# Three raw weight buffers, x's first chunk ahead of the first weights, and the last two column blocks computed token-major

## The chip, the core and the metric

The kernel runs on one NeuronCore of a Trainium2 chip: TensorE (PE, with its weight loads shown as PEld), VectorE (DVE), ScalarE (ACT), GpSimd (POOL) and SyncE (SP), which issues most of the DMA transfers. All five work through their own queue of instructions in order and wait for each other on semaphores. The metric is the device time of one execution in microseconds (us). The kernel before takes 1832.29 us, the median of three runs (1831.8 to 1832.62).

## What is computed

A two-layer encoder trunk on 512 tokens of width 1024, all in float32. Each layer mixes the tokens in three ways in parallel (differential attention, a depthwise convolution module, 2-D neighbourhood attention), merges them with sigmoid gates, then applies a gated feed-forward block and a gated per-layer input embedding. Cut to the frame:

```python
for i in range(DEPTH):
    h = rmsnorm(x, norm_mix[i])
    qa, ka, va, glu_in, qc, kc, vc, gates = split(h @ w_in[i])
    ya = diff_attention(qa, ka, va, ...)
    yb = conformer_conv(glu_in, ...)
    yc = neighbourhood_attention(qc, kc, vc, rpb[i])
    x = x + (ga * (ya @ w_br_a[i]) + gb * (yb @ w_br_b[i]) + gc * (yc @ w_br_c[i])) @ w_o[i]
    h = rmsnorm(x, norm_ffn[i])
    x = x + (silu(h @ w_ffn_gate[i]) * (h @ w_ffn_up[i])) @ w_ffn_down[i]
    h = rmsnorm(x, norm_ple[i])
    x = x + sigmoid(h @ w_ple_gate[i]) * (p[i] @ w_ple_in[i])
return rmsnorm(x, norm_final)
```

## The kernel before

**Layout.** Activations lie channel-major: a chunk is a [128 channels, 512 tokens] tile, and eight chunks make x. A block of 128 output channels is one accumulation in a PSUM bank. Every operand is split into a high part and a low remainder (`split`, L160: an ACT copy to the rounded type, then a DVE subtraction), and each product is three matmuls, high x high, high x low, low x high (`mm3`, L173; the three lines are L175 to L177). A full block is 8 chunks x 3 matmuls of 512 columns.

**Weights.** `weights` (L164) loads one block of up to 512 KB into a raw tile (tag `wr`, two buffers) from SP's queue, then splits it into `wh` and `wl` (three buffers each). A new load into `wr` waits until DVE's subtraction has read the raw tile that held the buffer before. The loads are put early in the program by a raised priority (`w_ahead`), and a scheduler orders the instructions of every engine but PE, whose order is written out by hand. SP's queue is strictly in order: what stands behind a waiting load waits too. Beside the weights it carries the biases, the rope tables and the small copies that `stack` (L611) makes inside the chip to build the stacked operands (`natten_qk`, `natten_x`, `diff_qk`) of the attention scores.

**Opening** (`opening`, L307). Ten warm-up matmuls on zeros run while the first data arrives. Then the first four blocks of the convolution's input are computed chunk by chunk (k = 0 to 7), so that x and the weights may arrive in pieces: weight columns 0 to 255 (for k = 0 and 1) in tiles `t`, 256 to 511 in `rp`, 512 to 1023 in `e`. x's chunk 0 and 1 are issued from ACT's queue (L315, L317), the rest and all weight pieces from SP's. For k = 0, `operand` (L257) makes the high part on ACT and the low one on DVE.

**Middle.** Neighbourhood attention (`natten_in`, `natten_unit`), differential attention, gates and convolution run interleaved; the convolution's 31 taps are DVE work placed between. Scratch tiles have the tag `t` (8 buffers), row tiles (broadcast norms, rope tables) the tag `r` (4).

**End** (`ple`, L949, and `final`, L995). In the last layer the blocks m = 0 to 6 of the gated embedding are computed channel-major; then `final` does block 7 in two halves of 256 tokens. PE turns the finished chunks, scaled by the final gain, back to token-major (`turn`, four transposes a time). Sums of squares per token are matmuls with a column of ones (`total`), the root is a POOL power (`column`), and DVE and ACT scale the turned tiles into one row tile for each 128 tokens, which SP stores with one 512 KB transfer (`store`, L1046).

## Time and profile before

| what | value |
|---|---|
| median of the runs | 1832.29 us (1831.8 to 1832.62) |
| the profiled execution, its own time | 1832.66 us |
| its span, first to last instruction | 1830.6 us |
| granted TensorE clock, mean | 0.998 |
| HBM read, written | 180.79 MB, 7.34 MB |
| DMA busy, hardware queue 1 | 37.5% of 16 engines |
| POOL busy | 23.6 us (1%) |
| costliest group: PE L175 `ffn_mm<-wo_h,ffn_wh`, 704 matmuls | 274.2 us |
| costliest on DVE: the convolution's taps, L158 `conv_z` | 179.4 us (240 x 748 ns) |
| costliest on ACT: the split L141 `ffn_wh<-ffn_wr` | 144.0 us (152 x 949 ns) |

The span is 2.1 us shorter than the execution's own time; the rest lies around it. In the views, a row of the timeline begins with the start and the duration in us, then engine, line, operation and tiles (`out<-in`), then how often; in square brackets stands the idle time before it and what ended it. In the views of waits the numbers are the total in us, how often, and the longest. A matmul's duration covers its way through the array, so consecutive matmuls overlap: what one costs is the distance between two starts. A window's row gives the busy time of PE, PEld, DVE, ACT and POOL, the granted PE clock, the DMA share and GB/s.

### The profile page before, as it was taken

To read this page: it belongs to the slowest core of one execution; us is meant where nothing else is said; L and a number is where in the kernel's file an instruction comes from. 1 tells how busy PE (TensorE), PEld (TensorE's weight loads), DVE (VectorE), ACT (ScalarE), POOL (GpSimd) and SP (SyncE) were. 2 spreads that over 40 slices of the span, in tenths; PEclk is the share of its full clock that TensorE was granted. 3 is DMA by queue.
4 is the path that set the end of the run, shared out by engine and by line. 5 is a ranking of instruction groups with operands and counts; after the bars stand their busy time and mean duration, and the time that the engine had idled before them with its cause. 6 is when DMAs were issued, how large, how long until landed. Compare 5 with 4: busy or idle time off the path is not lost.

```text
span 1830.6 us, 23574 instructions
## 1 busy us (share of the span) xinstructions
PE 1815.6 (99%) x8796; PEld 1524.3 (83%) x8796; DVE 1190.5 (65%) x1917; ACT 764.8 (42%) x1330; POOL 23.6 (1%) x56
## 2 busy tenths in 40 slices
PE   9999999999999999999999999999999999999998
PEld 7888888888888888888888888888878888888887
DVE  6888887887644434445777878888775444344455
ACT  5476555325432222233535755552353322232344
POOL 0000000000000000000000000000000000000000
PEclk9999999999999999999999999999999999999999
DMA  5565541334422232223436655322353222322232
GB/s 176 176 191 167 144 135 41 109 101 156 146 98 99 82 102 103 99 81 113 152 121 203 183 156 145 103 75 93 107 193 104 99 97 79 117 92 99 84 107 102
DMA packets 88225, 221.13 MB, mean 121 GB/s; under 512 B 12080, under 2 KB 19376, under 8 KB 88112
## 3 DMA queue, kind: packets, MB, share of 16 engines
q1 hardware_dynamic: 87536, 218.94, 37.5%
q8 instruction: 70, 1.15, 0.2%
q10 hardware_dynamic: 576, 0.69, 0.1%
q14 instruction: 43, 0.35, 0.1%
HBM read 180.79 MB, written 7.34 MB: 103 GB/s over the span
## 4 chain that ended last, share of the span: by engine, by line
PE 93%; DVE 2%; DMA 2%; ACT 2%; issue 1%; DVEq 0%; ACTq 0%; SPq 0%; POOLq 0%; POOL 0%
PE ffn_mm L175 13%; PE ffn_mm L177 13%; PE ffn_mm L176 13%; PE mergea_mm L176 2%; PE mergea_mm L175 2%; PE mergea_mm L177 2%; PE diff_sc L757 2%; PE gatec_mm L175 2%; PE gatec_mm L176 2%; PE gatec_mm L177 2%; PE ple_mm L177 2%; PE ple_mm L175 2%; PE ple_mm L176 2%; PE wo_mm L176 2%; PE wo_mm L177 2%; PE diff_mm L175 2%
## 5 line engine op out<-in xcount | busy, mean ns | idle before, releaser
L141 ACT ACTIVATE ffn_wh<-ffn_wr 128x1024 fp32r<-128x1024 f32 (+1 forms) x152 | 144.0, 949 | 513.9 <-issue 367.8
L175 PE MATMUL ffn_mm<-wo_h,ffn_wh 128*128 128x512 f32 x704 | 274.2, 390 | 0.0
L177 PE MATMUL ffn_mm<-wo_h,ffn_wl 128*128 128x512 f32 x704 | 273.9, 389 | 0.0
L176 PE MATMUL ffn_mm<-wo_h,ffn_wh 128*128 128x512 f32 x704 | 273.9, 389 | 0.0
L155 DVE TENSOR_TENSOR ffn_wl<-ffn_wr,ffn_wh 128x1024 fp32r<-128x1024 f32 (+1 forms) x152 | 164.7, 1085 | 129.2 <-ACT ffn_wh L141 129.2
L158 DVE SCALAR_TENSOR_TENSOR conv_z<-glu_z,pre_par,conv_z 128x512 f32<-128x512 f32 x240 | 179.4, 748 | 3.0
L177 PEld LDWEIGHTS ffn_mm<-wo_h,ffn_wl 128*128 128x128 f32 x704 | 132.1, 188 | 27.5
L176 PEld LDWEIGHTS ffn_mm<-wo_h,ffn_wh 128*128 128x128 f32 x704 | 132.1, 188 | 27.4
L175 PEld LDWEIGHTS ffn_mm<-wo_h,ffn_wh 128*128 128x128 f32 x704 | 132.1, 188 | 27.3
L155 DVE TENSOR_TENSOR ffn_t<-ffn_t,ffn_mm 128x512 f32<-128x512 f32 x44 | 30.3, 688 | 114.8 <-PE ffn_mm L177 114.8
L155 DVE TENSOR_TENSOR ffn_t<-ffn_mm,wo_r 128x512 f32<-128x512 f32 x44 | 30.4, 691 | 110.3 <-PE ffn_mm L177 110.3
L141 ACT ACTIVATE mergea_wh<-mergea_wr 128x1024 fp32r<-128x1024 f32 (+1 forms) x32 | 27.1, 848 | 96.6 <-PE mergea_mm L176 70.8
L175 PE MATMUL ffn_mm<-ffn_z,ffn_wh 128*128 128x512 f32 x160 | 62.2, 389 | 0.0
L176 PE MATMUL ffn_mm<-ffn_z,ffn_wh 128*128 128x512 f32 x160 | 62.2, 389 | 0.0
L177 PE MATMUL ffn_mm<-ffn_z,ffn_wl 128*128 128x512 f32 x160 | 62.2, 389 | 0.0
L175 PE MATMUL ffn_mm<-ffn_y,ffn_wh 128*128 128x512 f32 x160 | 62.2, 389 | 0.0
L176 PE MATMUL ffn_mm<-ffn_y,ffn_wh 128*128 128x512 f32 x160 | 62.2, 389 | 0.0
L177 PE MATMUL ffn_mm<-ffn_y,ffn_wl 128*128 128x512 f32 x160 | 62.2, 389 | 0.0
L141 ACT ACTIVATE diff_a<-diff_sc,diff_s 128x512 f32<-128x512 f32 x32 | 22.0, 689 | 61.8 <-DVE diff_s L848 61.8
L848 DVE TENSOR_REDUCE diff_s<-diff_sc 128x1 f32<-128x512 f32 x64 | 41.9, 685 | 5.9 <-PE diff_sc L757 5.8
L155 DVE TENSOR_TENSOR wo_x<-wo_x,ffn_mm 128x512 f32<-128x512 f32 x32 | 22.0, 687 | 31.5 <-PE ffn_mm L177 31.5
L141 ACT ACTIVATE natten_wh<-natten_wr 128x1024 fp32r<-128x1024 f32 x24 | 25.4, 1056 | 37.4 <-issue 18.0
(583 smaller groups left out, 4628.6 us busy)
## 6 DMA issues: line engine op xcount, KB each, us to landing
ffn_wr<-w_fg SPq DMA_DIRECT2D x44, 512.0 KB, 3.2
ffn_wr<-w_fu SPq DMA_DIRECT2D x44, 512.0 KB, 3.1
ffn_wr<-w_fd SPq DMA_DIRECT2D x32, 512.0 KB, 3.4
natten_wr<-w_in SPq DMA_DIRECT2D x16, 512.0 KB, 3.7
natten_b<-bias SPq DMA_DIRECT2D x32, 256.0 KB, 3.3
diff_wr<-w_in SPq DMA_DIRECT2D x16, 512.0 KB, 3.5
gatec_wr<-w_in SPq DMA_DIRECT2D x16, 512.0 KB, 4.0
gateb_wr<-w_in SPq DMA_DIRECT2D x16, 512.0 KB, 3.3
```

The source lines that it names most:

```text
L141: i = self.nc.scalar.activation(out, in_, func, **kw)
L155: return self.nc.vector.tensor_tensor(out, a, b, op)
L158: return self.nc.vector.scalar_tensor_tensor(out, a, s, b, op0, op1)
L175: mm(out, wh, ah, start=first, stop=False)
L176: mm(out, wh, al, start=False, stop=False)
L177: mm(out, wl, ah, start=False, stop=last)
L757: self.nc.tensor.matmul(out, st4[:, u, qs], st[:, ks], start=n == 0, stop=n == 1)
L848: nc.vector.tensor_reduce(out=m[:, u:u + 1], in_=sc, op=ALU.max, axis=AX.X, negate=True)
```

## The change

`build`: the raw weight tag `wr` gets three buffers for two, `t` seven for eight, `r` three for four. `opening`: x's chunk 0 is the first transfer of SP's queue; the weight pieces are columns 0 to 127 (k = 0 alone), 128 to 511 (k = 1 to 3) and 512 to 1023; the first of the small pieces, x's chunk 1 and the rest of the parameters go to ACT's queue; `operand` of chunk 1 now stands ahead of the `rp` pieces. `ple`: the last layer's loop stops after block 5, and the new `gains` turns the last two blocks' final gains into rows. `final` computes blocks 6 and 7 together, token-major: the activations (128 tokens) are the stationary operand, and the two blocks' weights, loaded side by side, the moving one of 256 columns; four token tiles follow each other. The sums of squares of the last two blocks come from a DVE reduction along the rows; each row tile is stored in two transfers of 256 KB, one from ACT's queue and one from SP's.

```diff
--- before.py
+++ after.py
@@ -288,8 +288,8 @@
     def build(self):
         nc, tc, a = self.nc, self.tc, self.a
-        self.bufs = dict(wr=2, wh=3, wl=3, h=8, qk=2, kh=2, v=4, pt=2, y=5, z=5, x=4, t=8, rp=4,
-                         e=4, a=3, r=4, ss=1, sm=8, rc=4, b=2, s=8)
+        self.bufs = dict(wr=3, wh=3, wl=3, h=8, qk=2, kh=2, v=4, pt=2, y=5, z=5, x=4, t=7, rp=4,
+                         e=4, a=3, r=3, ss=1, sm=8, rc=4, b=2, s=8)
         self.bg, self.w_ahead = BG, 400
         self.pbufs = dict(mm=3, sc=2, tr=2, av=1)
         with tc.tile_pool(name="sb", bufs=1) as self.pool, \
@@ -310,20 +310,18 @@
         self.parts = self.sb("par", [P, PAR], bufs=1)
         self.small()
         mix = slice(0, KD)
+        xc = [t for _ in range(KD // 2) for t in self.parts_of("x", [512], 2)]
+        nc.sync.dma_start(xc[0], a["xT"][0])
         nc.scalar.dma_start(self.parts[:, mix], a["par"][:, mix])
-        xc = [t for _ in range(KD // 2) for t in self.parts_of("x", [512], 2)]
-        nc.scalar.dma_start(xc[0], a["xT"][0])
         self.consts()
-        nc.scalar.dma_start(xc[1], a["xT"][1])
-        nc.scalar.dma_start(self.parts[:, KD:], a["par"][:, KD:])
         warm = self.ps("av")
         for _ in range(WARM):
             nc.tensor.matmul(warm, self.zero_r, self.zero_r[:, None, :].to_broadcast([P, 4, P]),
                              start=True, stop=True)
         blocks = []
         lows = [t for _ in range(2) for t in self.parts_of("qk", [1024], 2, F32R)]
-        raws = {"t": [self.sb("t", [P, 256]) for _ in range(4)],
-                "rp": [self.sb("rp", [P, 256]) for _ in range(4)],
+        raws = {"t": [self.sb("t", [P, P]) for _ in range(4)],
+                "rp": [self.sb("rp", [P, 384]) for _ in range(4)],
                 "e": [self.sb("e", [P, 512]) for _ in range(4)]}
         for m in range(4):
             src = a["w_in"][0, (OFF_GLU + (0 if m % 2 else CB)) // P + m // 2]
@@ -335,17 +333,19 @@
         for k in range(KD):
             if k > 1:
                 nc.sync.dma_start(xc[k], a["xT"][k])
-            pieces = {0: (0, 256, "t"), 2: (256, 512, "rp"), 4: (512, 1024, "e")}
+            pieces = {0: (0, P, "t"), 1: (P, 512, "rp"), 4: (512, 1024, "e")}
             if k == 0:
-                h.append(self.operand(xc[k], self.par(0, "mix", k), FIRST[0][k]))
+                nc.scalar.dma_start(raws["t"][0], blocks[0][0][:, 0:P])
+                nc.scalar.dma_start(xc[1], a["xT"][1])
+                nc.scalar.dma_start(self.parts[:, KD:], a["par"][:, KD:])
+            h.append(self.operand(xc[k], self.par(0, "mix", k), FIRST[0][k]))
             if k in pieces:
                 c0, c1, tag = pieces[k]
                 for m, (src, wh, wl, _) in enumerate(blocks):
                     raw = raws[tag][m]
-                    nc.sync.dma_start(raw, src[:, c0:c1])
+                    if k or m:
+                        nc.sync.dma_start(raw, src[:, c0:c1])
                     self.split(wh[:, c0:c1], wl[:, c0:c1], raw)
-            if k:
-                h.append(self.operand(xc[k], self.par(0, "mix", k), FIRST[0][k]))
             s = slice(k * P, k * P + P)
             for src, wh, wl, ps in blocks:
                 self.mm3(ps, wh[:, s], wl[:, s], *self.halves(h[k]), k == 0, k == KD - 1)
@@ -951,7 +951,7 @@
         nc, i = self.nc, self.i
         last = i == L - 1
         hn, st = [], []
-        for m in range(KD - last):
+        for m in range(KD - 2 * last):
             g = self.sb("t", [P, 512])
             if m < EARLY:
                 pi = self.embedded(m)
@@ -970,6 +970,8 @@
                 self.act(g, g, AF.Sigmoid, table="sigmoid")
             self.ready(gate)
+            if last and m == 3:
+                self.gains()
             if m >= EARLY:
                 pi = self.ps("sc")
                 self.gemm(pi, self.a["w_pi"][i, m], pairs)
@@ -987,96 +989,127 @@
             self.ready(rest)
         if last:
-            return self.final(h, x[KD - 1], pairs, hn, st[0])
+            return self.final(h, x[KD - 2:], pairs, hn, st[0])
         self.i = i + 1
         self.main_norm(st[0], (3, 2), x=x)
         return hn
+    def gains(self):
+        o = self.ps("tr", (P, 2, P))
+        for u in range(2):
+            g = self.par(0, "fin", KD - 2 + u)
+            self.nc.tensor.transpose(o[:, u], g.to_broadcast([P, P]), self.ident)
+        self.gain = self.sb("b", [P, 2 * P])
+        self.act(self.gain, o.rearrange("p a b -> p (a b)"), AF.Copy)
     def final(self, h, x, pairs, hn, most):
...
+        nc, i, mm = self.nc, self.i, self.nc.tensor.matmul
+        def side_by_side(src, k0, n):
+            raw = self.sb("wr", [P, n, 2, P])
+            hi, lo = self.sb("wh", [P, n, 2 * P], F32R), self.sb("wl", [P, n, 2 * P], F32R)
+            with self.tc.high_priority(offset=self.w_ahead):
+                for b in range(2):
+                    nc.sync.dma_start(raw[:, :, b], src[KD - 2 + b][:, k0 * P:(k0 + n) * P]
+                                      .rearrange("p (a b) -> p a b", b=P))
+                self.split(hi, lo, raw.rearrange("p a b c -> p a (b c)"))
+            return [(hi[:, k], lo[:, k]) for k in range(n)]
+        wi = side_by_side(self.a["w_pi"][i], 0, 2)
+        wg = side_by_side(self.a["w_pg"][i], 0, 4) + side_by_side(self.a["w_pg"][i], 4, 4)
+        rbs = self.col
+        rows = [self.sb("y", [P, D]) for _ in range(4)]
+        def products(out, ws, acts, t, ks):
+            ts = slice(t * P, (t + 1) * P)
             for k in ks:
...
+                hi, lo = self.halves(acts[k])
+                a, z = k == 0, k == len(acts) - 1
+                mm(out, hi[:, ts], ws[k][0], start=a, stop=False)
+                mm(out, hi[:, ts], ws[k][1], start=False, stop=False)
+                mm(out, lo[:, ts], ws[k][0], start=False, stop=z)
+        def turn(tag, src, t):
             o = self.ps(tag, (P, 4, P))
...
+            for u, a in enumerate(src):
+                nc.tensor.transpose(o[:, u], a[:, t * P:(t + 1) * P], self.ident)
             return o.rearrange("p a b -> p (a b)")
...
+        def finish(t):
+            g = self.sb("t", [P, 256])
+            self.act(g, pgs[t], AF.Sigmoid, table="sigmoid", scale=rbs[:, t:t + 1])
+            self.tt(g, g, pis[t], ALU.mult)
+            v = self.sb("a", [P, 256])
+            self.tt(v, g, pair[t][:, 256:], ALU.add)
+            q = self.sb("t", [P, 256])
+            s = self.sb("s", [P, 1])
+            nc.vector.tensor_tensor_reduce(
+                out=q, in0=v, in1=v, scale=1.0, scalar=0.0, op0=ALU.mult, op1=ALU.add,
+                accum_out=s)
+            ms = self.sb("sm", [P, 1])
+            self.stt(ms, s, 1.0 / D, part[:, t:t + 1], ALU.mult, ALU.add)
+            col = self.sb("rc", [P, 1])
+            nc.gpsimd.tensor_tensor(col, ms, self.power[:, 0:1], ALU.pow)
+            vs.append(v)
+            columns.append(col)
+        def store(t):
+            col, two = columns[t], pair[t]
+            r, out = rows[t], self.a["out"][t * P:(t + 1) * P]
+            self.act(r[:, 0:512], low[t], AF.Copy, scale=col)
+            nc.scalar.dma_start(out[:, 0:512], r[:, 0:512])
+            self.stt(r[:, 768:], vs[t], col, self.gain, ALU.mult, ALU.mult)
+            nc.vector.tensor_scalar(r[:, 512:768], two[:, 0:256], col, None, ALU.mult)
+            nc.sync.dma_start(out[:, 512:], r[:, 512:])
+        pair, low, pgs, vs, columns = [], [], [], [], []
+        places = ("av", "mm", "av", "sc")
+        def inputs(t):
+            pis.append(self.ps("sc", (P, 256)))
+            products(pis[t], wi, pairs, t, range(2))
+        def chunks(t):
+            pair.append(turn("tr", (hn[4], hn[5], x[0], x[1]), t))
+        pis = []
+        for t in range(4):
+            pg = self.ps("mm", (P, 256))
+            if t == 0:
+                inputs(0)
+                inputs(1)
+            products(pg, wg, h, t, range(4))
+            if t == 1:
+                chunks(0)
+            if t in (1, 2):
+                low.append(turn(places[t - 1], hn[0:4], t - 1))
+            products(pg, wg, h, t, range(4, 6))
+            if t == 1:
+                sums = self.ps("mm", (P, 4))
+                for c in range(4):
+                    mm(sums[:, c:c + 1], most[:, c * P:(c + 1) * P], self.ones[:, 0:1],
+                       start=True, stop=True)
+                part = self.sb("sm", [P, 4])
+                nc.vector.tensor_scalar(part, sums, 1.0 / D, EPS, ALU.mult, ALU.add)
+            if t:
+                chunks(t)
+            if t > 1:
+                inputs(t)
+            products(pg, wg, h, t, range(6, 8))
+            pgs.append(pg)
+            if t == 1:
+                finish(0)
+            if t:
+                finish(t)
+            if t in (1, 2):
+                store(t - 1)
+        for t in (2, 3):
+            low.append(turn(places[t], hn[0:4], t))
+            store(t)
         return None
```

More of the change, by code (lines that the diff above doesn't have):

```diff
@@ L993, in ple @@
         return hn
-    def final(self, h, x, pairs, hn, most):
-        nc, i, m = self.nc, self.i, KD - 1
-        wg = self.weights(self.a["w_pg"][i, m], 1024)
-        wi = self.weights(self.a["w_pi"][i, m], 256)
-        hn.append(self.sb("h", [P, 512]))
-        g = self.sb("t", [P, 512])
-        sq = self.sb("t", [P, 512])
-        sums = self.ps("tr", (P, 2, 4))
-        def products(out, w, acts, half, ks):
-            s = slice(half * 256, half * 256 + 256)
-            for k in ks:
-                a = acts[k] if isinstance(acts[k], tuple) else (acts[k][:, 0, :], acts[k][:, 1, :])
-                c = slice(k * P, (k + 1) * P)
-                self.mm3(out, w[0][:, c], w[1][:, c], a[0][:, s], a[1][:, s],
-                         k == 0, k == len(acts) - 1)
-        def total(n, src, cs):
-            for c in cs:
-                nc.tensor.matmul(sums[:, n, c:c + 1], src[:, c * P:(c + 1) * P],
-                                 self.ones[:, 0:1], start=True, stop=True)
-        def turn(tag, n, c):
+    def gains(self):
[5 more added lines that the diff above has]
+        self.act(self.gain, o.rearrange("p a b -> p (a b)"), AF.Copy)
@@ L1021, in turn @@
             o = self.ps(tag, (P, 4, P))
-            for u in range(4):
-                nc.tensor.transpose(o[:, u], hn[4 * n + u][:, c * P:(c + 1) * P], self.ident)
+            for u, a in enumerate(src):
+                nc.tensor.transpose(o[:, u], a[:, t * P:(t + 1) * P], self.ident)
             return o.rearrange("p a b -> p (a b)")
-        def gate(pg, half):
-            s = slice(half * 256, half * 256 + 256)
-            self.tt(g[:, s], pg, self.rb[:, s], ALU.mult)
-            self.act(g[:, s], g[:, s], AF.Sigmoid, table="sigmoid")
@@ L1031, in rest @@
-        def rest(pi, half):
-            s = slice(half * 256, half * 256 + 256)
-            self.tt(g[:, s], g[:, s], pi, ALU.mult)
-            self.tt(x[:, s], x[:, s], g[:, s], ALU.add)
-            self.act(sq[:, s], x[:, s], AF.Square)
-            self.act(hn[m][:, s], x[:, s], AF.Copy, scale=self.par(0, "fin", m))
-        def column(half):
-            cs = slice(2 * half, 2 * half + 2)
-            ms = self.sb("sm", [P, 2])
-            self.stt(ms, sums[:, 1, cs], 1.0 / D, part[:, cs], ALU.mult, ALU.add)
-            col = self.sb("rc", [P, 2])
-            nc.gpsimd.tensor_tensor(col, ms, self.power[:, 0:2], ALU.pow)
-            return col
@@ L1046, in store @@
-        def store(c, col, tiles):
-            r = rows[c]
-            nc.vector.tensor_scalar(r[:, 0:512], tiles[0], col, None, ALU.mult)
-            self.act(r[:, 512:1024], tiles[1], AF.Copy, scale=col)
-            nc.sync.dma_start(self.a["out"][c * P:(c + 1) * P, :], r)
-        rows = [t for _ in range(2) for t in self.parts_of("qk", [1024], 2)]
-        pg = [self.ps("mm", (P, 256)), None]
-        products(pg[0], wg, h, 0, range(8))
-        gate(pg[0], 0)
-        pi = [self.ps("sc", (P, 256)), None]
@@ L1057, in final @@
-        products(pi[0], wi, pairs, 0, range(2))
-        rest(pi[0], 0)
-        total(0, most, range(4))
-        part = self.sb("sm", [P, 4])
-        nc.vector.tensor_scalar(part, sums[:, 0, :], 1.0 / D, EPS, ALU.mult, ALU.add)
-        lows = [turn("av", 0, 0), turn("tr", 0, 1)]
-        pg[1] = self.ps("mm", (P, 256))
-        products(pg[1], wg, h, 1, range(6))
-        total(1, sq, (0, 1))
-        col = column(0)
-        products(pg[1], wg, h, 1, range(6, 8))
-        gate(pg[1], 1)
-        pi[1] = self.ps("sc", (P, 256))
@@ L1070, in final @@
-        products(pi[1], wi, pairs, 1, range(2))
-        rest(pi[1], 1)
-        for c in range(2):
-            store(c, col[:, c:c + 1], (lows[c], turn("mm", 1, c)))
-        lows = [turn("sc", 0, 2), turn("sc", 0, 3)]
-        total(1, sq, (2, 3))
-        col = column(1)
-        highs = [turn(t, 1, 2 + c) for c, t in enumerate(("mm", "av"))]
-        for c in range(2):
-            store(2 + c, col[:, c:c + 1], (lows[c], highs[c]))
+        def finish(t):
[15 more added lines that the diff above has]
+            columns.append(col)
```

## The prediction

> **What bounds the kernel now.** I read the page first. TensorE is busy nearly all the span, and the chain that ended last lies on it:

> ```profile
> PE 1815.6 (99%) x8796; PEld 1524.3 (83%) x8796; DVE 1190.5 (65%) x1917; ACT 764.8 (42%) x1330; POOL 23.6 (1%) x56
> PE 93%; DVE 2%; DMA 2%; ACT 2%; issue 1%; DVEq 0%; ACTq 0%; SPq 0%; POOLq 0%; POOL 0%
> ```

> So the time is PE's matmuls plus the little time in which PE stands, plus what follows its last matmul. 1830.6 - 1815.6 = 15.0 us is all that is not covered. Where? PE's waits, longest first:

> ```profile
> PE natten_sc L757 <- DMA natten_x<-natten_t: 2.0, 1, 2.0
> PE pre_mm L175 <- ACT pre_y L141: 1.4, 1, 1.4
> PE natten_tr L678 <- DVE natten_pt L155: 1.3, 2, 0.6
> PE pre_av L321 <- DVE pre_zeror L381: 1.1, 1, 1.1
> ```

> Six smaller ones add 2.8 us; the rest, about 6 us, lies behind the last matmul (1824.7 to 1830.6). No wait of the long feed-forward stage is in the list: raw weights do not hold PE there, whatever SP and ACT wait for. Since busy PE need not be fast PE, I then looked at the granted clock:

> ```profile
> 4.00:8.00 4.00, 2.59 (x8) 1.48 (x8) 1.62 (x4) 2.38 (x6) 0.00 (x0) 1.00 1.06 374
> 8.00:12.00 4.00, 4.00 (x13) 3.13 (x12) 3.93 (x11) 3.79 (x10) 0.00 (x0) 0.57 0.95 252
> ```

> PE has 1.4 us without work in the first of these windows, and in the second the clock is at about half. In the timeline the starts of the 512-column matmuls are 0.43 us apart from 8.46 to 11.44, and 0.227 afterwards: 7 matmuls lose 0.2 us each, 1.4 us in all. The change touches three places: the opening, the raw buffers, the end.

> **Opening.** The chain of waits there:

> ```profile
> 1.17 4.05 DMA pre_x<-xT
> 5.24 0.33 ACTq L318
> 5.62 0.72 ACT glu_v L141
> 6.34 0.31 ACT pre_y L141
> 6.70 0.50 PE pre_mm L175
> ```

> x's chunk 0 lands at 5.22, the parameters' issue (L318) costs ACT another 0.4, then one operand and one weight piece are made. In the changed order chunk 0 is SP's first transfer, issued at 0.74. The first SP transfer of before (128 KB) took 2.6 us; twice the bytes at the 374 GB/s of the window adds 0.35: it lands near 3.7. The small parameter transfer (issued 0.73, 2.8 us to landing) lands at 3.5; the second parameter transfer, which waits for it on ACT, is issued by 3.9. The ACT operand then starts near 3.9 instead of 5.62, ends at 4.6, and a 128-column piece (0.28, the 128x128 rows of `natten_v`) makes the first weights ready near 4.9. The last warm-up matmul starts at 4.90, so the first real one can start at about 5.2 instead of 6.70: 1.5 us. The low halves follow on DVE 0.76 behind ACT (6.38 after 5.62), ready near 5.4, so chunk 0's first three matmuls lose some 0.2 instead of the 0.47 of before (6.70 to 7.85 for three). The gap of 1.4 us is then almost closed, and I take the half-clock stretch behind it to vanish with it: 12 matmuls x 0.227 = 2.7, and chunk 1 starts at 5.2 + 2.7 + 0.2 = 8.1 instead of 11.44. Gain 3.3 us.

> Is chunk 1 fed by then? It now needs the 384-column pieces: chunks 0 and 1 of x (512 KB), small pieces (256), `rp` pieces (768), parameters (161) are 1.7 MB, which at 374 GB/s from about 2.5 us on is through at 7.1; the last of its four blocks is needed only at 8.1 + 9 x 0.227 = 10.1. ACT's work until then is 0.72 + 4 x 0.28 + 0.72 + 4 x 0.5, DVE's is similar: from 3.9, done by 8.5 and 9.4. Covered by some 0.7 us; without that cover chunk 1 waits for it. Bounds: 1.0 (fed late, half clock comes back) to 3.8.

> [...] The row speaks for the gap: nothing else precedes the half clock, and it occurs nowhere else before the last matmul.

> **Three raw buffers.** A load for raw tile n now waits for the subtraction of tile n-3 instead of n-2. In feed-forward this frees SP and saves nothing, since PE does not wait there. One place differs. SP's queue:

> ```profile
> 76.50 0.60 SPq L617 DMA_DIRECT2D natten_x<-natten_t  x1
> 78.57 0.33 SPq L169 DMA_DIRECT2D natten_wr<-w_vc  x1
> 78.95 0.46 SPq L617 DMA_DIRECT2D natten_x<-natten_t  x1
> ```

> Two copies of `stack` are made from the same finished tile; the first goes at 76.50 and lands after 2.4 us, the second stands behind a weight load that waits for DVE's subtraction (77.32 + 1.23), goes at 78.95 and takes 5.4 beside that load. It lands at 84.36, and PE's scores wait for it from 82.33: the 2.0 us of the list. In the changed queue that load stands ahead of both `natten_x` copies and waits for the subtraction before (71.53 + 1.23 = 72.76), so it is gone when the copies are ready; the second is issued near 77.1 and lands by 80 to 81. Gain 2.0 us, bounds 0 to 2.0. The other waits of the middle (3.4 us) I leave: two of them, 0.6 (`pin_sc`) and 0.5 (`wo_mm`), lie where the weights' round trip is on the chain, so up to 1.1 more may go. I went through SP's new order for weight loads moved ahead of small copies: the worst is the stack of the last attention head, held from 254.2 to 255.9, and PE reads it at 274. One `t` and one `r` buffer less: every row tile's predecessor is read long before (the rope tables are fetched while the last norm of the layer before is over), scratch tiles live a few us; I take 0, bound +0.7 (one wait of the 0.6 kind).

> **End.** From block 6's first matmul (1803.92) on, PE before starts its last product at 1820.26, 16.3 us later. Afterwards: 120 products of 256 columns at 0.12 = 14.4 (the same work: 30 x 0.227 + 60 x 0.12 before), 24 transposes at 0.11 = 2.6 (in front of the last product, 8 before), four ones-sums 0.9 (the same), seven switches at 0.1: 18.6 us. The last product is 2.3 us later. Then before:

> ```profile
> 1819.36 0.70 POOL L1043 TENSOR_TENSOR ple_rc<-ple_sm,pre_power 128x2 f32<-128x2 f32 x1 [40.87 <-DVE ple_sm L158]
> 1824.08 0.70 POOL L1043 TENSOR_TENSOR ple_rc<-ple_sm,pre_power 128x2 f32<-128x2 f32 x1 [4.03 <-DVE ple_sm L158]
> 1824.81 1.41 DVE L1048 TENSOR_SCALAR ple_qk<-ple_sc,ple_rc 128x512 f32<-128x512 f32 x2 [0.88 <-POOL ple_rc L1043]
> ```

> the last store is issued at 1826.29, 6.0 us after the last product's start. Afterwards the chain is shorter: product ends 0.28, sigmoid straight from PSUM 0.2 + 0.42, two DVE steps of 0.44, a row reduction 0.42 + 0.08 (the `natten_b` rows of L654), scale 0.17, POOL 0.07 + 0.70, two DVE steps 0.82: 4.0 us. The two cancel to about -0.3 + 0.6 of waiting between engines: issue at the same time within 0.5. What is left is the transfer: the last 512 KB took 3.2 us behind another of 512 KB; alone, one took 2.6; now two of 256 KB go side by side with nothing in front. Gain 0.6. The two gain transposes cost PE 0.2. Weights side by side load in 512-byte pieces, but some 10 us before use; their split waits for block 5's buffer, free at 1803.9 as in before (ACT 1803.94, DVE done 1806.27), and chunk 4 needs them at 1803.9 + 24 x 0.12 = 1806.8: covered by 0.5. Net -0.4, bounds -1.8 to +1.5.

> **Sum.** -3.3 - 2.0 - 0.4 = -5.7 against the profiled execution's 1832.66 (span 1830.6 and 2.1 around it), so 1827.0. That execution is 0.4 above the median of the runs: 1826.6. All bounds at their best: -3.8 - 3.1 - 1.8 = -8.7, 1823.6.

> **Rivals.** 0.2% (3.7 us) is about what a measurement tells from no change.
> 1. The half clock stays, because something other than the 1.4 us gap brings it: only the earlier start is won, 1.5 + 0.3 in the opening, sum -4.2, 1828.1. For it: this trace has one such stretch, so one case to judge by; against: it begins right behind the gap. Chance 0.12. [...]
> 2. The natten wait only changes its name (another copy or DVE is last): -3.7, 1828.6, on the edge. For it: DVE is over 90% busy in 130 to 150; against: only 6.9 of 10 us in 70 to 80, 6.5 in 80 to 90. Chance 0.10.
> 3. The opening is fed late, 512-byte pieces and 768 KB for chunk 1: opening 1.0, sum -3.4, 1828.9. Against: the byte count above. Chance 0.09. The change not doing what it says (the load still ahead of the copies, the opening bound by ACT): -1 to -2, chance 0.05.
> 4. Slower. Weight loads issued earlier run beside the stack copies of the 16 attention pairs and heads; a copy beside a load took 5.4 instead of 2.4. If eight of the places where PE now has slack under 1.5 us lose 1.5, that is +12, and without the 2.0 of natten -3.7: +8.3, 1840.6. It decides where copies land within 1.5 us of their scores; before, one place in 16 waits at all, and loads run beside copies already. Chance 0.06.

> Forecast 0.58. Faster by over 0.2%: 0.58 + 0.12 + half of rival 2 and some of 3, 0.78; same 0.14; slower 0.08. The range takes rivals 1 to 3: 1823.9 to 1830.5.

> **What would show it.** Right: first real matmul near 5.2 and chunk 1's at 8 with no half clock; no `natten_sc <- DMA` wait at 80; last store as far behind block 6 as before, span's end 0.5 nearer. Wrong: a window of clock near 0.5 after 8 us, a new PE wait on `pre_rp` or on stack copies, or PE waiting for `ple_wl` or `ple_tr` in the last 25 us.

## The result, and the profile after

The changed kernel takes 1825.82 us (median of 6 runs, 1824.07 to 1829.48) against 1832.05 for the kernel before beside it (6 runs, 1830.91 to 1834.95): ratio 0.9969, 95% interval 0.9955 to 0.9982, so 6.2 us faster; 1826.6 was forecast. In two later sets the same kernel had 1825.21 (ratio 0.9963, 0.9951 to 0.9976) and 1824.89 (0.9959, 0.9946 to 0.9971).

Parts 1 and 4 of the page after, from an execution of 1829.48 us (span 1827.5):

```profile
PE 1815.3 (99%) x8820; PEld 1527.3 (84%) x8820; DVE 1191.9 (65%) x1928; ACT 763.5 (42%) x1325; POOL 24.4 (1%) x58
PE 96%; DVE 2%; ACT 1%; issue 1%; DMA 0%; SPq 0%; DVEq 0%; POOLq 0%; ACTq 0%
```

By this page DMA has left the chain (2% before, 0% now), and PE is still nearly all of it. Its waits, in us in total, how often, and the longest:

```profile
PE natten_sc L757 <- DMA natten_qk<-natten_t: 2.1, 1, 2.1
PE natten_tr L678 <- DVE natten_pt L155: 1.3, 2, 0.6
PE pre_av L319 <- DVE pre_zeror L381: 1.1, 1, 1.1
PE natten_sc L757 <- DMA natten_x<-natten_t: 0.7, 1, 0.7
```

The opening's 1.4 (`pre_mm <- pre_y`) and the small waits of `pin_sc`, `wo_mm` and `ple` are gone. The 2.0 for a stack copy is gone from 82.3, but 2.8 for other copies of the same stack, those of the first scores, stand at 76.4 to 79.9. Windows of the same run (busy PE, PEld, DVE, ACT, POOL, then granted clock, DMA share, GB/s):

```profile
4.00:8.00 4.00, 4.00 (x13) 3.11 (x13) 1.78 (x6) 2.30 (x7) 0.00 (x0) 1.00 0.97 284
8.00:12.00 4.00, 4.00 (x18) 2.92 (x16) 3.55 (x9) 3.78 (x8) 0.00 (x0) 1.00 0.93 312
75.00:80.00 5.00, 2.19 (x9) 1.28 (x8) 2.70 (x7) 1.38 (x7) 0.00 (x0) 0.85 1.01 213
80.00:85.00 5.00, 5.00 (x13) 4.08 (x14) 1.03 (x5) 2.00 (x6) 0.00 (x0) 0.50 0.50 154
```

The opening has no gap, and its clock does not fall back. PE begins at half clock in both kernels (0.43 us between starts) and in this execution stays there until 6.86, in the kernel before until 4.70; no clock record lies ahead of these times, so the view's 1.00 at 4 to 8 hides it. At 75 to 80 PE works 2.19 of 5 us, and in the next five the clock is at half. The profile of the second set (after_again below, an execution of 1825.21) has the same waits, shorter, and no half clock:

```profile
75.00:80.00 5.00, 3.30 (x16) 2.35 (x15) 3.02 (x11) 1.97 (x8) 0.00 (x0) 1.00 0.87 231
80.00:85.00 5.00, 5.00 (x27) 4.22 (x26) 3.38 (x9) 4.18 (x12) 0.00 (x0) 1.00 0.54 150
```

Behind the first scores PE is 4.3 us later in the first profile than in this one, and the spans differ by 4.4: between these two executions this place is all of it. That it is what spreads the others from 1824 to 1829.5 is likely, but not shown. What holds the copies shows in SP's queue of the first profile (start, us, then the DMA that is issued):

```profile
67.49 1.20 SPq L617 DMA_DIRECT2D natten_qk<-natten_kh  x2
70.51 0.33 SPq L169 DMA_DIRECT2D natten_wr<-w_vc  x1
70.90 1.99 SPq L617 DMA_DIRECT2D natten_x<-natten_kh  x2
72.93 1.23 SPq L617 DMA_DIRECT2D natten_qk<-natten_t  x2
74.21 1.24 SPq L617 DMA_DIRECT2D natten_x<-natten_t  x2
```

DVE finished `natten_t`, the source of the last four, at 67.03. SP stands from 68.7 to 70.51 at the weight load, which waits for DVE's subtraction (69.26 + 1.23); the copies go after it. They are issued 2.3 us earlier than in the kernel before all the same (`natten_x <- natten_t` at 74.21 instead of 76.50), just as PE is 2.3 us early there. It is the landing that is late: 79.93 instead of 78.86, 5.7 us after the issue instead of 2.4, for a matmul that in the kernel before started at 78.90, with no slack. With three raw buffers the load ahead of these copies is `w_vc`'s instead of `w_in`'s, and from issue to landing it took longer (first line the kernel before, second the changed one; KB, us):

```profile
natten_wr<-w_in SPq DMA_DIRECT2D x1, 512.0 KB, 3.7
natten_wr<-w_vc SPq DMA_DIRECT2D x1, 512.0 KB, 6.6
```

In the other two profiles of the changed kernel it took 5.3 and 4.2, and PE's listed waits for the copies were 1.7 and 0.7; in e2_raw3, with the same order, 4.9 and 1.1. Of the profiles with two raw buffers, four have 3.7 to 3.9 for the load ahead, but e8_warm 5.9. So it is not shown that the third buffer makes that load slower, nor why it takes 4.2 to 6.6 us in three executions of one kernel.

Where the time came from, by the start of the same matmul in two traces (us earlier than in the kernel before; worked out from the rows of PE):

| place, time in the kernel before | after_again | e2_raw3, buffers alone |
|---|---|---|
| chunk 1 of the opening, 11.44 | 3.27 | 1.90 |
| first neighbourhood scores, 78.69 | 1.72 | 1.41 |
| second matmul of them, 78.90 | 0.73 | 0.53 |
| behind the old wait, 84.40 | 2.93 | 2.71 |
| `diff_sc`, 1130 | 4.17 | 3.85 |
| `pin_sc`, 1344 | 5.19 | 4.87 |
| `wo_mm`, 1371 | 5.91 | 5.58 |
| end of the span | 7.45 | 5.68 |

The tail of after, from its rows of ACT, DVE, POOL:

```profile
1820.55 0.47 ACT L141 ACTIVATE ple_t<-ple_mm,ffn_rc 128x256 f32<-128x256 f32 x1 [2.95 <-PE ple_mm L1035]
1822.74 0.54 POOL L1057 TENSOR_TENSOR ple_rc<-ple_sm,pre_power 128x1 f32<-128x1 f32 x1 [2.86 <-DVE ple_sm L158]
1823.32 0.49 DVE L158 SCALAR_TENSOR_TENSOR ple_y<-ple_a,ple_rc,ple_b 128x256 f32<-128x256 f32 x1 [0.72 <-POOL ple_rc L1057]
1824.03 0.34 ACTq L1065 DMA_DIRECT2D out<-ple_y  x1
```

Block 6's first matmul starts at 1802.52, the last product at 1820.23, the last store goes at 1824.2, the span ends at 1827.5: 25.0 us in all, 26.6 before.

### The profile page after: what moved, and what is told of

The parts are those of the page before. It is cut to its first block, busy times and chain, and to the rows that moved or that the text cites. A ratio compares the mean times of both kernels' runs of the same rounds, so it can differ in the third digit from the quotient of the medians.

```text
span 1827.5 us, 23665 instructions
## 1 busy us (share of the span) xinstructions
PE 1815.3 (99%) x8820; PEld 1527.3 (84%) x8820; DVE 1191.9 (65%) x1928; ACT 763.5 (42%) x1325; POOL 24.4 (1%) x58
## 4 chain that ended last, share of the span: by engine, by line
PE 96%; DVE 2%; ACT 1%; issue 1%; DMA 0%; SPq 0%; DVEq 0%; POOLq 0%; ACTq 0%
PE ffn_mm L175 13%; PE ffn_mm L177 13%; PE ffn_mm L176 13%; PE mergea_mm L175 2%; PE mergea_mm L177 2%; PE mergea_mm L176 2%; PE diff_sc L757 2%; PE gatec_mm L175 2%; PE gatec_mm L176 2%; PE gatec_mm L177 2%; PE gateb_mm L176 2%; PE gateb_mm L175 2%; PE gateb_mm L177 2%; PE wo_mm L176 2%; PE wo_mm L175 2%; PE wo_mm L177 2%
## 5 line engine op out<-in xcount | busy, mean ns | idle before, releaser
L141 ACT ACTIVATE ffn_wh<-ffn_wr 128x1024 fp32r<-128x1024 f32 (+1 forms) x152 | 144.3, 951 | 513.3 <-issue 382.8
L175 PE MATMUL ffn_mm<-wo_h,ffn_wh 128*128 128x512 f32 x704 | 274.2, 390 | 0.0
L155 DVE TENSOR_TENSOR ffn_wl<-ffn_wr,ffn_wh 128x1024 fp32r<-128x1024 f32 (+1 forms) x152 | 164.8, 1085 | 130.4 <-ACT ffn_wh L141 130.4
L158 DVE SCALAR_TENSOR_TENSOR conv_z<-glu_z,pre_par,conv_z 128x512 f32<-128x512 f32 x240 | 179.3, 747 | 2.9
L175 PEld LDWEIGHTS ffn_mm<-wo_h,ffn_wh 128*128 128x128 f32 x704 | 132.2, 188 | 27.3
L155 DVE TENSOR_TENSOR ffn_t<-ffn_t,ffn_mm 128x512 f32<-128x512 f32 x44 | 30.3, 688 | 114.8 <-PE ffn_mm L177 114.7
L155 DVE TENSOR_TENSOR ffn_t<-ffn_mm,wo_r 128x512 f32<-128x512 f32 x44 | 30.4, 692 | 109.7 <-PE ffn_mm L177 109.7
L141 ACT ACTIVATE mergea_wh<-mergea_wr 128x1024 fp32r<-128x1024 f32 (+1 forms) x32 | 27.1, 848 | 96.8 <-PE mergea_mm L176 70.8
L175 PE MATMUL ffn_mm<-ffn_z,ffn_wh 128*128 128x512 f32 x160 | 62.2, 389 | 0.0
L175 PE MATMUL ffn_mm<-ffn_y,ffn_wh 128*128 128x512 f32 x160 | 62.2, 389 | 0.0
L141 ACT ACTIVATE diff_a<-diff_sc,diff_s 128x512 f32<-128x512 f32 x32 | 22.0, 687 | 60.6 <-DVE diff_s L848 60.6
L155 DVE TENSOR_TENSOR wo_x<-wo_x,ffn_mm 128x512 f32<-128x512 f32 x32 | 22.0, 688 | 31.4 <-PE ffn_mm L177 31.4
L141 ACT ACTIVATE natten_wh<-natten_wr 128x1024 fp32r<-128x1024 f32 x24 | 25.4, 1059 | 39.7 <-issue 17.7
```

The source lines that it names most:

```text
L141: i = self.nc.scalar.activation(out, in_, func, **kw)
L155: return self.nc.vector.tensor_tensor(out, a, b, op)
L158: return self.nc.vector.scalar_tensor_tensor(out, a, s, b, op0, op1)
L175: mm(out, wh, ah, start=first, stop=False)
```

## The experiments

Twelve kernels ran in four sets of five rounds each. Differences are between medians of one set: to the kernel before (1831.97, 1831.44, 1832.20 and 1832.29 in the four sets), and to the changed kernel where it ran in the same set.

**e1_open**, the kernel before with the new `opening` alone (its part of the diff above).

> The kernel before with the changed opening alone. Theory A (the opening's gain is eaten at the first neighbourhood scores): in the profile PE's first real matmul is at 5.5 and chunk 1 starts at 8.9 instead of 11.4, so PE runs some 2.3 us early up to 76, but the copies of the stack (natten_x <- natten_t) land no earlier than in the kernel before (80 to 84.5), so PE's waits of natten_sc on DMA grow from 2.0 to 4 us or more and the offset against the kernel before is back to within 0.7 us by 86. Time -0.7 to +1 us (1831.3 to 1833). Rival C (the parts add, the gain of the opening stays): the waits stay near 2 us, time -2.3 us, 1829.7.

1830.55, -1.4 us (ratio 0.9991, 0.9982 to 1.0000): between the two, and the interval reaches no change. Theory A's reason falls: the stack copies do come earlier with the opening (the last one issued at 77.00 instead of 78.95), and PE's wait stays at 1.8. But this time the half clock follows, from 83.63 to 87.04, and PE's lead of 2.0 us at 82.4 is 0.4 behind that stretch. The opening itself had kept only that much: PE's lead of 3.25 at chunk 1 is 2.0 by 15 us, since the operands of chunk 1 and 2 come late.

**e2_raw3**, the buffer counts alone.

```diff
-        self.bufs = dict(wr=2, ..., t=8, rp=4, ..., r=4, ...)
+        self.bufs = dict(wr=3, ..., t=7, rp=4, ..., r=3, ...)
```

> The kernel before with only the numbers of buffers changed (three raw weight buffers, one row tile and one scratch tile less). Theory A: the weight load no longer stands between the two stack copies, PE reaches the scores no earlier than in the kernel before (78.7), so the 2.0 us wait at 82.3 falls to under 0.7, and the waits of pin_sc (0.6) and wo_mm (0.5) late in the kernel go too: -2.0 to -3.5 us, 1828.5 to 1830. Rival B (the copies are bound by the transfers beside them, not by the order of the queue): the copies beside the weight load take over 5 us as in the changed kernel, a wait of 1 us or more on a stack copy stays at 78 to 84, and the gain is under 1.5 us.

1826.73, -5.2 us (0.9976, 0.9967 to 0.9985), more than either theory said. Its waits on stack copies:

```profile
PE natten_sc L757 <- DMA natten_x<-natten_t: 0.7, 1, 0.7
PE natten_sc L757 <- DMA natten_qk<-natten_t: 0.4, 1, 0.4
```

1.1 in place of 2.0, and no half clock follows. The table above has the rest: `pin_sc` and `wo_mm` give 1.7, small places between 84 and 1130 another 1.1. The 1.9 of its opening are not the edit's: the gap was 1.3 us instead of 1.4, and the clock stayed up (0.23 us between starts from 7.48 to 8.40).

**e3_end**, the new `ple`, `gains` and `final` alone.

> The kernel before with only the token-major end (the last two blocks, the gains of the last norm, the sums along rows). All theories: nothing changes before 1800. From the first matmul of block 6 to the span's end 25.0 us instead of 26.6: -1.65 us, 1830.4 (1829.9 to 1831.2). The prediction's own step says -0.4: 1831.6.

1829.69, -2.3 us (0.9993, 0.9984 to 1.0001): the interval reaches no change, so it is the profile that shows the gain. Counted from PE's last feed-forward instruction to the end of the span its profile takes 47.17 us, as the changed kernel's does, and the kernel before 48.55: -1.4.

**e4_later**, the changed kernel with the first pair's scores later.

```diff
-            self.later(self.natten_unit(...), 5, 1)
+            self.later(self.natten_unit(...), 7 if pr == self.i == 0 else 5, 1)
```

> The changed kernel with one number more: in layer 0 the scores of the first pair of heads are called two ticks later, so that some 5 us of other PE work runs ahead of them. Theory A (PE stands 2.8 us because it reaches the scores before the stack copies have landed, and the idle time lets the clock fall in some executions): the waits of natten_sc on DMA near 77 to 79 fall under 0.5, no half clock follows, the runs near 1829 go, and the median is 2 to 3.5 us under the changed kernel: 1822.3 to 1823.8. Rival B (layer 0's attention is bound by the chain through ACT, DVE and SP from the opening on, so that whatever PE does first it waits at the next place): the wait turns up behind the scores (natten_tr, natten_av, or the next pair), median within 1 us of the changed kernel, 1825 to 1826.5.

1827.02, -4.9 us, 0.5 above what rival B gave, but its mechanism: the waits for copies are gone, and PE now waits behind the scores, 1.9 for `natten_pt`, 1.4 for `natten_y`, 1.1 for `natten_a`, all made by DVE (1.3, 0.5 and none in the changed kernel's profiles), and the half clock comes at 104 instead.

**after_again**, the changed kernel once more, as partner.

> The changed kernel once more, as the partner of the three beside it on the same chip: 1825.8 (its median before), and in its profile PE waits of 2 to 3 us on the stack copies between 76 and 80. If an idle stretch of 1.4 us or more inside one cell of the clock's 3.41 us grid is what halves the clock, the next cell is at half whenever the copies' wait falls whole into one cell, and not where the grid cuts it.

1825.21, -6.2 us. The waits were 0.9 and 0.8, no more than 1.2 us idle in one cell, and no half clock.

**e5_noopen**, the changed kernel with the old `opening`.

> The changed kernel with the opening of the kernel before. Buffers alone gave -5.2 and the end alone -2.3 against the kernel before. Theory A (the opening gives nothing on top of the buffers, since PE only comes earlier to stack copies that are held by SP's queue): -5.5 to -7.5 us against the kernel before, not slower than the changed kernel by more than 0.5, PE's wait for the copies near 1 us in the profile. Rival C (the opening's gain stays in the changed kernel): slower than the changed kernel by 1.4 to 2.5 us.

1826.41, -5.0 us, and 1.2 slower than the changed kernel (1.5 between the two spans): between the theories, and the five times of each overlap. Against after_again PE is 2.9 us behind at chunk 1, 2.4 behind ahead of the scores and 1.5 behind after the stack, where its wait for the copies is 0.7 instead of 1.7. Against after_third, where the load ahead of the copies took 4.2 us, it is 2.4 behind at chunk 1, 2.1 ahead of the scores and still 2.0 after the stack. So how much of the opening's gain is waited away at the copies goes by the execution. This opening, too, had its share of the grid: PE stays at half clock until 10.39.

**e6_ahead**, the changed kernel with the order of one queue turned.

```diff
-                        self.nc.sync.dma_start(st[r:r + 64, u]..., part[...]...)
+                        with self.tc.high_priority(offset=(60 if self.lead else 0)):
+                            self.nc.sync.dma_start(st[r:r + 64, u]..., part[...]...)
```

`self.lead` is set for pair 0 of layer 0.

> The changed kernel with one order turned: in layer 0's first pair the five stack copies that stand behind the weight load of w_vc go ahead of it on SP's queue. Theory A1 (the copies, ready at 67.0, stand behind a load that waits until 70.5 for DVE's subtraction): the last natten_x <- natten_t is issued near 72 instead of 74.8 and lands by 78, PE's waits of natten_sc on DMA fall from 2.8 us to 1 us or less, no half clock follows there, and the median is 2 to 3 us under the changed kernel's: 1823 to 1824. Rival A2 (the copies are bound by the DMA engines' bandwidth): issued earlier, they land no earlier than 79, the wait stays over 2 us, time within 0.7 us of the changed kernel. Rival A3 (the load that now goes 2 us later is the next to be late): a PE wait on weights (natten_mm on natten_wl) of 1 us or more, time unchanged or longer.

1825.80, -5.6 us: no gain. Yet the first half of A1 holds. SP's queue:

```profile
68.44 0.55 SPq L621 DMA_DIRECT2D natten_x<-natten_t  x1
69.04 1.24 SPq L621 DMA_DIRECT2D natten_qk<-natten_t  x2
70.32 1.23 SPq L621 DMA_DIRECT2D natten_x<-natten_kh  x2
71.60 1.31 SPq L621 DMA_DIRECT2D natten_x<-natten_t  x1
73.01 3.29 SPq L169 DMA_DIRECT2D natten_wr<-w_vc  x2
```

The last copy goes at 71.6 to 72.9 instead of 74.8 to 75.5, no wait of `natten_sc` on DMA is left, and PE is 2.0 us ahead of after_again at 78. So it was the load ahead of them in SP's queue that held the copies (rival A2 had them land no earlier than 79; the last one lands at 75.3), by SP's standing and by its own way to landing, which this run does not tell apart. No wait on weights appears either (rival A3). The 2.0 are given back between 88 and 97. DVE's rows there:

```profile
92.75 0.73 DVE L158 SCALAR_TENSOR_TENSOR conv_z<-glu_z,pre_par,conv_z 128x512 f32<-128x512 f32 x1
93.40 0.41 DVE L155 TENSOR_TENSOR natten_y<-natten_av,natten_y 64x256 fp32r<-64x256 f32 x1
93.73 0.74 DVE L158 SCALAR_TENSOR_TENSOR conv_z<-glu_z,pre_par,conv_z 128x512 f32<-128x512 f32 x1
94.50 0.42 DVE L155 TENSOR_TENSOR natten_y<-natten_y,natten_av 64x256 fp32r<-64x256 f32 x1
94.85 0.74 DVE L158 SCALAR_TENSOR_TENSOR conv_z<-glu_z,pre_par,conv_z 128x512 f32<-128x512 f32 x1
95.62 0.69 DVE L155 TENSOR_TENSOR natten_pt<-natten_tr,natten_pt 128x512 fp32r<-128x512 f32 x1
```

DVE has no pause here, and the convolution's taps (0.74 each), put into its queue as background, stand ahead of `natten_y` and `natten_pt`, for which PE's next products wait. PE's place at the front of the stage is no longer what sets its end.

**e8_warm**, the kernel before with `WARM = 14` for 10.

> The kernel before with 14 warm-up matmuls instead of 10, so that PE's gap of 1.4 us ahead of the first real matmul is filled and nothing else is changed. If the gap brings the half clock in the opening: the first real matmul stays at 6.7 (the operands come no earlier), no cell at half follows, chunk 1 starts at 9.5 instead of 11.4, and the time is up to 1.9 us shorter, less what the wait for the first stack copies takes back: -0.7 to -1.9 us, 1830.1 to 1831.3. If the half clock has another cause, the cell at half stays and the time is that of the kernel before within 0.5.

1831.75, +0.3 us (0.9999, 0.9990 to 1.0008). Its one profile agrees with the gap as the cause; compare the windows of the kernel before in the prediction.

```profile
4.00:8.00 4.00, 4.00 (x13) 2.71 (x13) 1.76 (x5) 2.51 (x7) 0.00 (x0) 1.00 1.05 374
8.00:12.00 4.00, 4.00 (x19) 3.33 (x18) 4.00 (x11) 4.00 (x10) 0.00 (x0) 1.00 0.85 251
```

With the gap filled the clock stays up, and chunk 1 starts at 9.77 instead of 11.44, though the first real matmul starts only 0.13 earlier. This alone does not settle it: in e2_raw3 the gap is not filled, and the clock stays up too. That profiled execution is the fastest of its eleven (1828.67); the medians show no gain, and the interval leaves room for 1.8. What a half cell in the opening costs in the end stays open.

**e9_order**, the kernel before, two raw buffers, with e6_ahead's edit.

> The kernel before, with its two raw weight buffers, and only the order turned that the prediction named: the first pair's last natten_x <- natten_t copy goes ahead of the weight load of w_vc on SP's queue, instead of behind it. The prediction's step: the last copy is issued near 77.1 instead of 78.95 and lands by 80 to 81, PE's 2.0 us at 82.3 vanish, no half clock follows there, time -2.0 us or up to -3.5 with the half cell that the wait brings in most executions: 1828 to 1829.5. Rival (the wait only changes its name; three buffers bring their 5 us elsewhere): another copy or the weights are last, a wait of 1 us or more stays between 78 and 86, time within 1 us of the kernel before.

1829.68, -2.5 us (0.9986, 0.9977 to 0.9995), just above the expected range. The last copy is issued at 77.35, ahead of the load at 78.67; no wait on a stack copy is left in its list, and PE is 2.0 us earlier at 84.4. The edit moves other copies of the pair as well (the first `natten_x <- natten_t` goes at 73.26 instead of 76.50). With that said, this is the prediction's step by itself, and it is right. In this profile, of an execution of 1832.22, only 0.4 of the lead is left at 1371 (0.8 goes at `wo_mm` near 467); the gain to the end rests on the medians. The three buffers change this order and, by the medians of the two sets, 2.7 us more.

**e7_bg2**, e6_ahead with two background taps for three.

```diff
-BG = dict(glu=2, natten=3, diff=1, gatec=2, ...)
+BG = dict(glu=2, natten=2, diff=1, gatec=2, ...)
```

> The changed kernel with the first pair's copies ahead of the load, as in the run before, and two instead of three of the convolution's multiply-adds (conv_z, 0.74 us of DVE each) let in behind every projection of the neighbourhood heads. Theory A (with the copies in time PE runs into DVE's queue at 90 to 97, where conv_z stands ahead of natten_pt and natten_y and gives the 1.5 us back): PE's lead of 1.5 to 2 us over the changed kernel at 88 is still over 1 us at 100, and the median falls by 1 to 2 us, to 1823.8 to 1824.8. Rival B (the convolution's work is only late elsewhere: it is needed by the merge, and DVE is full in 130 to 150 in any case): the lead is gone by 150 or by the merge at 1370, median within 0.7 us of the changed kernel (1825.2) or above it.

1826.94, -5.3 us. Both halves are seen: PE's lead over after_again is 1.4 at 104, 2.4 at 145 and 2.0 at 224, so DVE's queue was the cause; then the taps are late:

```profile
PE conv_tr L536 <- DVE conv_ss L155: 2.8, 2, 1.4
```

1.4 us in each layer, where the convolution's norm needs all taps.

**after_third** and **e10_gatec3**: the partner, and e7_bg2 with `gatec=3`, so that the eight taps are made between 180 and 300, where DVE has slack (in e7_bg2 25.1, 27.0, 26.0 and 22.0 us busy in its four stretches of 30).

> The changed kernel as partner on the same chip: 1825.2 to 1825.8, the medians of its two sets of runs.

> The changed kernel with the first pair's copies ahead of the load, two multiply-adds of the convolution per neighbourhood projection instead of three, and the eight so left out per layer let in at the eight projections of gatec (three each instead of two), where DVE has slack (22 of 30 us in 270 to 300 in the run before). Theory A (the convolution came 5.9 us of DVE late at conv_tr, 1.4 us of PE per layer, and that alone ate the lead of 2.0 us): no wait of conv_tr on conv_ss, the lead of 2 us at 220 is still there at 430 and a further 1 us comes in layer 1: median 2 to 3 us under the changed kernel, 1822.5 to 1823.8. Rival B (another place takes it back): a new wait of 1 us or more between 230 and 430, median within 0.7 us of the changed kernel.

1824.89 (1824.44 to 1825.00) and 1823.49 (1822.60 to 1824.43): -7.4 and -8.8 us, ratios 0.9959 and 0.9951 (0.9937 to 0.9965). The five runs of each do not overlap, 1.4 us apart. Of e10's waits none on a copy or on `conv_ss` is left:

```profile
PE pre_av L320 <- DVE pre_zeror L382: 1.1, 1, 1.1
PE natten_av L703 <- DVE natten_y L155: 0.4, 1, 0.4
```

It is the fastest kernel of the study. PE's lead over after_third is 1.9 us at 199 and 1.6 from 224 to 430, and in layer 1 nothing more is won: 1.4 from 1126 to 1700.

## Why the prediction was right, and where it was not

The total was right (-5.7 forecast, -6.2 measured, -6.2 and -7.4 later), but its terms were not; their errors cancel, and that the total comes so near is in part luck. One of its own signs of being wrong did come: a new PE wait on stack copies.

**Opening, -3.3.** Seen where it was put: the first real matmul starts at 5.2 to 5.5 (forecast 5.2), chunk 1 at 8.2 to 8.9 (forecast 8.1), no fall back to half clock. Rival 3 (fed late) is there in small: from chunk 1 to 15 us the lead over the kernel before shrinks by 0.3, 0.5 and 0.3 us in the three profiles of the changed kernel, to 2.3, 2.8 and 2.4, and by 1.3 in e1_open. And by the medians only 1.2 (e5_noopen) to 1.4 (e1_open) reaches the end, neither clear of the noise. The step that failed is that a gain at 8 us was carried to the end of the span unchanged. Besides, part of the 3.3 was the half clock of one profiled execution: with the same old opening, e2_raw3's chunk 1 starts at 9.54, 1.9 us earlier than in the kernel before.

**Raw buffers, -2.0.** The queue did what was said, the copies landed in time for the old arrival of PE ("lands by 80 to 81": 79.9), and e9_order shows the 2.0 in isolation. The step that failed is "gain 2.0" in the whole change: PE's arrival was taken from the trace of before, though the opening moves it from 78.7 to 76.4, and only the copy of the second scores was followed. The copies of the first scores had no slack, and behind a load that took 4.2 to 6.6 us instead of 3.7 they landed late. From ahead of the scores to behind them the changed kernel gains 0.3 us on the kernel before in after_again and 1.2 in after_third, and loses 3.5 in the first profile, half clock included; e2_raw3 gains 0.8. Rival 2 is what happened at this place: the wait only changed its name, 2.8, 1.7 and 0.7 us in three profiles. It was given 0.10; the time did not come out at its 1828.6 because two other terms, the other waits and the end, were too small.

**"The other waits of the middle I leave."** The bound of 1.1 for `pin_sc` and `wo_mm` was put at nothing. These two places gave 1.7 us in after_again and in e2_raw3, and small ones before 1130 another 1.2 and 1.1. Of the profiles with two raw buffers most have some of these two waits, but not e8_warm's (kernel before 1.1 together, e1_open 1.2, e3_end 0.4, e9_order 1.9, e8_warm 0); those of the seven kernels with three buffers have none. That fits the third buffer as the cause of the missing waits; since e8_warm lacks them too, it is not shown. **One `t` and one `r` less at nothing**: no PE wait in the profiles' lists is for either.

**End, -0.4.** From block 6 on 1.6 us were won, 1.4 with the gain transposes, forecast at 0.2, which lie before it. The chain behind the last product is 4.0 us, as forecast. Two terms were mis-sized: sums and switches, of which the 0.1 for a switch was an estimate, took 0.7 instead of 1.6 (1820.23 - 1802.52 - 120 x 0.12 - 24 x 0.11), so that the last issue came 0.7 us earlier and not at the same time, and from it to the span's end 3.3 us pass instead of 4.27, a gain of 0.9 and not 0.6.

**Rival 1, the half clock.** That the gap of 1.4 us brings the half clock rests on the list below, where the cells ahead of a half one were idle for 1.41 to 2.08 us; e8_warm, with the gap filled and the clock at 1.00 from 8 to 12, agrees. **Rival 4**, copies made late by loads: it is seen at the one place above (5.7 us instead of 2.4), not at the sixteen.

## What to carry to other kernels

An edit's gain is good only up to the next place where the engine meets something that does not move with it: work out again who comes last there, with the new arrival time, for every edit that lies before. When a wait is removed and the time does not move, follow the lead of the same instruction between two traces until it is lost; here that named the load ahead of the copies in SP's queue, then the background taps in DVE's, and at last the place with slack for them. The first edit alone and the first two won nothing; all three won 1.4 us.

## What the runs showed of the hardware

```
kernel       cell from  idle in it  next cell
before           4.70      1.41     half
e9_order         4.33      1.65     half
e3_end           3.99      1.76     half
e1_open         80.22      1.78     half
e3_end          82.50      1.92     half
after           75.12      1.95     half
e4_later       100.66      2.08     half
before          83.21      1.19     full
after_again     76.61      1.18     full
e2_raw3          4.21      1.26     full
e7_bg2         407.72      1.42     full
e7_bg2        1312.24      1.23     full
```

Of the cells in which PE's work ends, one with 1.94 us idle (e10_gatec3) and one with 1.36 (after) were followed by a full one, and one with 1.39 (e2_raw3) by a half one, so 1.4 is no sharp limit. The wait of 2.0 us of the kernel before brought no half clock: a cell's border at 83.21 cuts it, with 0.82 us idle in the cell ahead of it and 1.19 in the one behind. By the grid a half cell costs PE up to 1.7 us of work (half of 3.413); in the kernel before's, seven matmuls started 0.43 us apart instead of 0.227, 1.4 us. After a half cell less was enough: 0.86 us of idle time in the cell from 78.54 of the changed kernel was followed by another half one, as was 0.68 at the start of e5_noopen; 0.47 at the start of e3_end was followed by a full one.

Small copies inside the chip were no fixed cost: the two copies of 128 KB of `natten_x <- natten_t` took 2.4 and, beside a weight load, 5.4 us in the kernel before, and 5.7 (median of the two) in the changed one, where four other copies and two weight loads of 512 KB were issued from 70.5 to 76.3. In the same order they took 4.6 in after_again and 3.3 in after_third. In the changed kernel the copies landed in the order of their issue, one after the other behind the load (77.12, then 77.39 to 80.57).
